# Output projection and second norm with features on partitions, late modulation as columns, residual turned back by VectorE

## The chip, the core and the metric

The kernel runs on one core of one Trainium2 chip. The metric is device time in microseconds (us) of one launch. Engines have their usual names: PE is TensorE, DVE VectorE, ACT ScalarE, POOL GpSimd, SP the engine on whose queue nearly all transfers are issued.

## The reference, cut to what matters

One layer of a residual block for 1024 tokens of 1024 features, float32, with a mixer in front and a SwiGLU behind:

```
mod = silu(c) @ w_ada + b_ada                       # six rows of 1024
shift1, scale1, gate1, shift2, scale2, gate2 = split(mod, 6)
h = rms_norm(x, norm1_w) * (1 + scale1) + shift1
x = x + gate1 * (concat[gated delta rule(h), short conv(h)] @ w_out)    # w_out 1024 x 1024
h = rms_norm(x, norm2_w) * (1 + scale2) + shift2
x = x + gate2 * ((silu(h @ w_gate) * (h @ w_up)) @ w_down)              # 2816 inner features
out = rms_norm(x, norm_f_w)
```

## The kernel before, in words

Every float32 product is made of three passes: each operand is split into a rounded part ("hi", made by ACT) and a rest ("lo", source minus hi, made by DVE), and hi·hi, hi·lo and lo·hi are added in a PSUM bank of 128 x 512. A group of 8 blocks of 128 for the contraction is therefore 24 matmuls.

The program has three stretches.

The **planned stretch** runs from the start to the first half of the output projection. Its steps are tasks in Python threads; `Sim` estimates when each engine could take which step and so writes the order of every queue. Here are the combined projection (`fill`, PE's steady work), the delta rule in two halves of 512 tokens (`gdn`), and the modulation. Of the latter, `ada` and `gate5` make gate1, shift2, scale2 and gate2 as rows: `ada_rows` loads blocks of `w_ada`, adds them up on DVE weighted with `c_act`, and adds over the partitions by two matmuls against `ones`. `w_unit` prepares `w_out`: it multiplies the weight's columns by gate1 and splits. At the end `fill` runs the output projection of the first 512 tokens, with tokens on the partitions of the result: eight groups of 24 matmuls, added to the residual `x2` by `ev_o`. `norm0` saves `x2` to `x2_scr`, takes each token's root mean square by ACT (a sum along the row) and scales.

The **hand-ordered stretch** follows: every engine does its instructions in the order in which the code is written. `w_out_tile(t, ch)` is one group of the projection of the second 512 tokens, `norm_tile` its norm. The SwiGLU wants features on partitions, so the normed rows are turned by PE: `first_half`, `inner_half` and `t_split` write four transposes of 128 x 128 into a bank, ACT takes hi from it, DVE lo.

The SwiGLU's two first products use Strassen-Winograd's seven products in place of eight over halves of tokens, features and columns: the operands of x are B11, B21, B22 and the sums T1 to T4, those of the weights A11, A12, A22 and the sums S1 to S4. `W[p]` holds the weights of pair p of column blocks (11 pairs), `run(p, s)` is step s of a pair: 24 matmuls. Pair 0 (before `for p in range(1, NP)`) also makes the operands from x: `t_split`, `t_high`, `t_low`, `t_sums`, `t_parts`; `part` splits the weights. `block(p, s)` is the other engines' work beside a step. The **third stretch**, the product with w_down, reads `x2` again from `x2_scr`; the change does not touch it.

An instruction that waits holds up all that stands behind it on its engine's queue, transfers on SP's too. Small tiles come from rings: `raw_t` takes one of five tiles of 128 x 512 in turn, so the sixth user waits until the first tile's last reader, which may be a transfer, is through.

Of the kernel before, what the change touches and what calls it, by code (L numbers as in the profile page):

```python
# [51 lines left out]
def kernel(  # L52
# [6 lines left out]
    w_ada: bass.AP,  # L59
    w_mod: bass.AP,  # L60
    b_ada: bass.AP,
# [49 lines left out]
    wada, wout = w_ada[0], w_out[0]  # L111
# [31 lines left out]
    x2_scr = drp.tile([NT, P, D], F32, name="x2_scr", tag="x2_scr")  # L143
    am_scr = drp.tile([NF // 2, 7, P, HT], F32, name="am_scr", tag="am_scr")
# [396 lines left out]
    mod_c = cst.tile([P, 16], F32, name="mod_c", tag="mod_c")  # L541
    s2c = cst.tile([P, KB], F32, name="s2c", tag="s2c")
    b2c = cst.tile([P, KB], F32, name="b2c", tag="b2c")
    db2 = cst.tile([P, 4], F32, name="db2", tag="db2")
    db3 = cst.tile([P, 2], F32, name="db3", tag="db3")
    su = []
# [161 lines left out]
    def setup():  # L708
        sim.wait(lambda: "loads0" in done)
        dma(ct, consts)  # L710
        dma(hv[:, 0:4], A_log[0].partition_broadcast(P))
        dma(hv[:, 4:8], dt_bias[0].partition_broadcast(P))
        wabr = raw((P, KB, 8))
        dma(flat(wabr), w_ab)
        DVE.tensor_copy(row_h, ct[:, 648:652])
# [83 lines left out]
    def h1_load():  # L799
        sim.wait(lambda: "loads0" in done)  # L800
        for j in range(4):
            t = xp.tile([P, 2, HT], F32, name=nm("xt"), tag="x", bufs=8)
            dma(t, x_t[2 * j:2 * j + 2].rearrange("k p c -> p k c"))
            x1t.append(t)
# [130 lines left out]
    def fill():  # L935
# [22 lines left out]
        for ch, us in ((1, us1), (0, us0)):  # L958
            for i in range(4):
                ps = bank(dense, "o")  # L960
                sl = slice(i * P, (i + 1) * P)
                for n, k in enumerate(KORD):
                    sim.wait(lambda: k in us and k in Y[0])
                    for m, (yi, ui) in enumerate(((0, 0), (0, 1), (1, 0))):
                        mm(ps, Y[0][k][yi][:, sl], us[k][ui], n == 0 and m == 0, n == KB - 1 and m == 2)
                sim.spawn(ev_o, PR["evac"], ps, i, ch)

    def ev_o(ps, t, ch):
        cs = slice(ch * HT, (ch + 1) * HT)
        sim.wait(lambda: ("x2", t) in done)  # L970
        DVE.tensor_tensor(x2[t][:, cs], x2[t][:, cs], ps, ALU.add)
        free(ps)
        done.add(("o", t, ch))

    def norm0(t):
        sim.wait(lambda: ("o", t, 0) in done and ("o", t, 1) in done and su and "row" in done and ("g5", 0) in done and ("g5", 1) in done)
        dma(x2_scr[t], x2[t])
        junk = raw((P, D), BF16)
        st = cst.tile([P, 4], F32, name=nm("st"), tag="n2", bufs=4)
        ACT.activation(junk, x2[t], AF.Square, scale=1.0 / 32.0, accum_out=st[:, 0:1])  # L980
        free(junk)
        POOL.tensor_scalar(st[:, 1:2], st[:, 0:1], EPS, None, ALU.add)
        rsqrt_pow(st[:, 2:3], st[:, 1:2], 1)
        DVE.scalar_tensor_tensor(x2[t], x2[t], st[:, 2:3], su[0][:, 0], ALU.mult, ALU.mult)
# [3 lines left out]
    def ada_rows(b, ch, ac=None, get=None):  # L988
        if ac is None:
            ac = wst.tile([P, HT], F32, name=nm("aacc"), tag="aacc", bufs=1)  # L990
        row = get is None
        get = get or raw
        c0 = b * D + ch * HT
        for kk in range(KB):
            r = get()
            dma(r, wada[kk * P:(kk + 1) * P, c0:c0 + HT])
            if kk == 0:
                DVE.tensor_scalar(ac, r, c_act[:, 0:1], None, ALU.mult)
            else:
                DVE.scalar_tensor_tensor(ac, r, c_act[:, kk:kk + 1], ac, ALU.mult, ALU.add)  # L1000
            free(r)
        hl = [raw(dtype=F32R) if row else gt("Tt", (P, HT), F32R) for _ in range(2)]
        esplit(ac, hl[0], hl[1])
        if not row:
            return hl
        ps = bank(chb, "ada")
        mm(ps, ones_r, hl[0], True, False)
        mm(ps, ones_r, hl[1], False, True)
        for t in hl:
            free(t)  # L1010
        return ps

    g5 = {}

    def gate5(ch):
        sim.wait(lambda: len(us0) == KB and len(us1) == KB and "row" in done)
        if 5 not in gates:
            g = gates[5] = wst.tile([P, D], F32, name=nm("gate"), tag="gate", bufs=1)
            dma(g, b_ada[0, 5 * D:6 * D].partition_broadcast(P))
        ac = gt("A", (P, HT)) if ch else None  # L1020
        g5[ch] = ada_rows(5, ch, ac, (lambda: gt("Tt", (P, HT))) if ch else raw)
        done.add(("g5", ch))
        if ch:
            free(ac)

    def ada():
        sim.wait(lambda: 1 in sc_)
        g = wst.tile([P, D], F32, name=nm("gate"), tag="gate", bufs=1)
        dma(g, b_ada[0, 2 * D:3 * D].partition_broadcast(P))
        for ch in range(2):  # L1030
            ps = ada_rows(2, ch)
            DVE.tensor_tensor(g[:, ch * HT:(ch + 1) * HT], g[:, ch * HT:(ch + 1) * HT], ps, ALU.add)
            free(ps)
        gates[2] = g
        for b in (3, 4):
            for ch in range(2):
                ps = ada_rows(b, ch)
                j = (b - 3) * 8 + ch * 4
                diag = wst.tile([P, 4, P], F32, name=nm("diag"), tag="aacc", bufs=1)
                DVE.tensor_tensor(diag, v3(ps, 4), bc1(ident, 4), ALU.mult)  # L1040
                free(ps)
                DVE.tensor_reduce(mod_c[:, j:j + 4], diag, mybir.AxisListType.X, ALU.add)
        DVE.tensor_tensor(mod_c, mod_c, bac[:, 24:40], ALU.add)
        DVE.tensor_copy(b2c, mod_c[:, 0:8])
        DVE.scalar_tensor_tensor(s2c, mod_c[:, 8:16], 1.0, n2c, ALU.add, ALU.mult)
        DVE.tensor_tensor(db2, b2c[:, 4:8], b2c[:, 0:4], ALU.subtract)
        done.add("mods")

    def mod_rows():
        sim.wait(lambda: "mods" in done and ("gdn", 1) in done)  # L1050
        su.append(gt("u", (P, 2, D)))
        for ch in range(2):
            dg = raw((P, 4, P))
            DVE.tensor_tensor(dg, bc1(ident, 4), bc2(s2c[:, 4 * ch:4 * ch + 4], P), ALU.mult)
# [8 lines left out]
            ecopy(su[0][:, 0, ch * HT:(ch + 1) * HT], ps)  # L1063
            free(ps)
        done.add("row")

# [299 lines left out]
    def w_unit(k, ch, take, out_):  # L1366
        r = raw()
        cs = slice(ch * HT, (ch + 1) * HT)
        dma(r, wout[k * P:(k + 1) * P, cs])
        if k < 4:  # L1370
            DVE.scalar_tensor_tensor(r, r, gnc, gates[2][:, cs], ALU.mult, ALU.mult)
        else:
            DVE.tensor_tensor(r, r, gates[2][:, cs], ALU.mult)
        hi, lo = take()
        esplit(r, hi, lo)
# [45 lines left out]
    def w_out_units():  # L1421
        sim.wait(lambda: 2 in gates and "loaded" in done and len(Y[0]) > 5)
# [973 lines left out]
```

## Time and profile before

| | us |
|---|---|
| median of 3 runs | 1159.89 (1158.71 to 1160.67) |
| profiled execution, first to last instruction | 1158.3 |
| PE busy in it | 1148.2 (99%) |
| DVE busy | 961.4 (83%) |
| ACT busy | 565.6 (49%) |
| first matmul of the second half's projection (`w_out_tile(4, 1)`) | 471.55 |
| first matmul of pair 0 / of pair 1 | 520.46 / 564.16 |

The profiled execution's own time isn't given apart; the nearest run lies 0.4 us above its span, the median 1.6 us. Rows of the timeline read: start, duration, engine, line, operation, what it writes<-what it reads, count, and in brackets the idle time before it and what ended that. A row with a count merges instructions that follow each other; they overlap in the pipeline, so the time from one row's start to the next row's start over the count is the cost of one.

### The profile page before, as it was taken

How to read it: one execution, taken by the hardware profiler on the slowest of the kernel's cores; microseconds unless marked ns; L12 is line 12 of the kernel's file. 1: busy time of each engine (PE TensorE's matmuls, PEld its weight loads, DVE VectorE, ACT ScalarE, POOL GpSimd, SP SyncE). 2: the span in 40 equal slices, each digit the busy share in tenths (PEclk: the TensorE clock that was granted, in tenths of full speed). 3: DMA queues.
4: the chain of work that ended last, by engine and by line, in shares of the span. 5: the costliest groups of instructions: out<-in, count | busy, mean ns of one | idle time of the engine just before them, and what ended most of it. 6: DMA issues, size and time to landing. Idle time of an engine off the chain costs nothing.

```text
span 1158.3 us, 16873 instructions
## 1 busy us (share of the span) xinstructions
PE 1148.2 (99%) x5682; PEld 967.1 (83%) x5682; DVE 961.4 (83%) x1820; ACT 565.6 (49%) x1244; POOL 62.3 (5%) x100
## 2 busy tenths in 40 slices
PE   8999999999999999999999999999999999999997
PEld 7888888988888988888888888888888888888886
DVE  7899988999988898669987778877887798688676
ACT  6678732559634543346434443434434455443344
POOL 2110100001101001100000000000000000000002
PEclk9999999999999999999999999999999999999999
DMA  9824456534225546432564457545654599869403
GB/s 363 324 76 143 117 166 174 182 120 138 88 66 164 165 158 210 169 92 72 173 218 163 138 191 231 171 137 175 232 192 143 174 333 394 309 207 337 144 30 146
DMA packets 127544, 209.19 MB, mean 181 GB/s; under 512 B 20577, under 2 KB 45153, under 8 KB 127457
## 3 DMA queue, kind: packets, MB, share of 16 engines
q1 hardware_dynamic: 122080, 204.90, 52.8%
q10 hardware_dynamic: 5376, 3.21, 0.9%
q8 instruction: 45, 0.74, 0.3%
q14 instruction: 43, 0.34, 0.1%
HBM read 153.01 MB, written 55.05 MB: 180 GB/s over the span
## 4 chain that ended last, share of the span: by engine, by line
PE 94%; DVE 3%; ACT 1%; DMA 1%; issue 0%; ACTq 0%; DVEq 0%
PE acc L89 36%; PE acc L448 25%; PE dn L89 17%; PE o L89 4%; PE o L448 3%; PE tr L89 1%; PE K L448 1%; PE A L448 1%; DVE xo L90 1%; PE ab L448 1%; PE w L448 1%; PE u L448 1%; PE kk L448 1%; PE qk L448 1%; DMA raw<-in_w_out_dram 0%; DVE raw L448 0%
## 5 line engine op out<-in xcount | busy, mean ns | idle before, releaser
L448 PE MATMUL acc<-h,u 128*128 128x512 f32 x1200 | 297.9, 397 | 0.0
L448 PEld LDWEIGHTS acc<-h,u 128*128 128x128 f32 x1200 | 220.0, 188 | 42.5 <-issue 0.5
L89 PE MATMUL acc<-h,hl 128*128 128x512 f32 x576 | 135.1, 390 | 0.0
L89 PE MATMUL acc<-T,hl 128*128 128x512 f32 x552 | 130.8, 390 | 0.0
L89 PEld LDWEIGHTS acc<-h,hl 128*128 128x128 f32 x576 | 107.4, 188 | 21.9
L89 PEld LDWEIGHTS acc<-T,hl 128*128 128x128 f32 x552 | 102.4, 188 | 20.4
L90 DVE TENSOR_TENSOR xo<-xo,dn 128x512 f32<-128x512 f32 x84 | 57.0, 684 | 42.3 <-PE dn L89 34.6
L89 PE MATMUL acc<-h,u 128*128 128x512 f32 (+1 forms) x480 | 91.8, 341 | 0.0
L89 PE MATMUL dn<-h,h 128*128 128x512 f32 x396 | 90.7, 389 | 0.0
L89 PEld LDWEIGHTS acc<-h,u 128*128 128x128 f32 x480 | 78.3, 189 | 11.7
L89 PEld LDWEIGHTS dn<-h,h 128*128 128x128 f32 x396 | 74.3, 188 | 15.4
L90 DVE TENSOR_TENSOR cc<-cc,acc 128x512 f32<-128x512 f32 x66 | 41.4, 645 | 32.0 <-PE acc L89 32.0
L448 ACT CAST u<-raw 128x512 fp32r<-128x512 f32 x58 | 35.9, 621 | 56.9 <-PE acc L448 55.1
L448 DVE TENSOR_TENSOR u<-raw,u 128x512 fp32r<-128x512 f32 x82 | 56.1, 685 | 4.0 <-ACT u L448 3.5
L89 PE MATMUL acc<-T,u 128*128 128x512 f32 x240 | 56.0, 389 | 0.0
L448 DVE SCALAR_TENSOR_TENSOR cv<-pr,cols_a,cv 128x512 f32<-128x512 f32 x72 | 53.8, 756 | 0.3
L89 PEld LDWEIGHTS acc<-T,u 128*128 128x128 f32 x240 | 45.1, 188 | 9.3
L90 ACT CAST h<-rw 128x512 fp32r<-128x512 f32 x57 | 32.7, 618 | 41.3 <-PE dn L89 34.6
L90 ACT CAST hl<-S 128x512 fp32r<-128x512 f32 x44 | 25.3, 623 | 56.2 <-DVE S L90 56.2
L90 ACT ACTIVATE cc<-cc 128x512 f32<-128x512 f32 x33 | 20.9, 633 | 64.0 <-DVE cc L90 64.0
L90 ACT CAST u<-R 128x512 fp32r<-128x512 f32 (+1 forms) x60 | 34.2, 585 | 35.3 <-DVE R L90 34.2
L90 DVE TENSOR_TENSOR hl<-S,hl 128x512 fp32r<-128x512 f32 x44 | 28.5, 687 | 26.3 <-ACT hl L90 26.3
(377 smaller groups left out, 2145.1 us busy)
## 6 DMA issues: line engine op xcount, KB each, us to landing
raw<-in_w_in_dram SPq DMA_DIRECT2D x82, 256.0 KB, 3.3
am_scr<-cc SPq DMA_DIRECT2D x77, 256.0 KB, 4.3
raw<-in_w_ada_dram SPq DMA_DIRECT2D x56, 256.0 KB, 3.1
rw<-am_scr SPq DMA_DIRECT2D x55, 256.0 KB, 5.0
rw<-bm_scr SPq DMA_DIRECT2D x53, 256.0 KB, 5.1
bm_scr<-raw SPq DMA_DIRECT2D x51, 256.0 KB, 5.5
R<-in_w_gate_dram SPq DMA_DIRECT2D x22, 512.0 KB, 4.3
R<-in_w_up_dram SPq DMA_DIRECT2D x22, 512.0 KB, 5.5
```

What stands on the lines that cost most here:

```text
L89: return call(*a, **k)
L90: ins = call(*a, **k)
L448: ins = call(*a, **k)
```

## The change

- The output projection is turned: the weight is the stationary operand and y the moving one, so features are on the partitions of the result (`w_out_t(m, b)`; m is a block of 128 features). Still 24 matmuls a group and 8 groups for each 512 tokens.
- gate1, shift2, scale2 and gate2 are made as columns on DVE alone (a product with a running sum, from a transposed `w_mod`), without PE; only gate2 is spread to rows (`row`). gate1 is applied when a group leaves PSUM (`ev_o`, `evict`); `w_unit` only splits.
- The norm now sums over partitions: ACT squares, DVE adds the eight blocks (`sq`), PE adds over partitions by four matmuls with one moving column (`row_sums`), the root is taken on POOL or ACT (`row_root`), a diagonal of it is spread over partitions by a float32 matmul (`row_bc`), and DVE multiplies each block by it (`scale`).
- All of PE's transposes of x are gone (80). Operands are made in the order "scale, hi, lo" block after block (`h_first`, `t_make`).
- The residual is needed with tokens on partitions only at the end. For the first half DVE turns each block in 32 x 32 squares (`turn0`) and four transfers of 32-element runs put the squares in their place in `x2_scr`; for the second half the blocks are saved (`x2t_scr`) and turned one a pair during pairs 2 to 9 (`turn_load`, `turn1`).
- Pair 0 gets an order of its own, with the norm's two short PE steps put between its matmuls (`hooks`).

```diff
-        for ch, us in ((1, us1), (0, us0)):
-            for i in range(4):
...
-                        mm(ps, Y[0][k][yi][:, sl], us[k][ui], n == 0 and m == 0, n == KB - 1 and m == 2)
+        for m in M_ORD:                       # (4, 5, 6, 7, 0, 1, 2, 3)
...
+                    mm(ps, us[k][ui][:, sl], Y[0][k][yi], n == 0 and j == 0, n == KB - 1 and j == 2)
+            sim.spawn(ev_o, PR["evac"], ps, m)
+    def ev_o(ps, m):
+        x_ = x2[m][:, 0:HT]
+        DVE.scalar_tensor_tensor(x_, ps, g1c[:, m:m + 1], x_, ALU.mult, ALU.add)
...
+        ACT.activation(r, x_, AF.Square, scale=1.0 / 32.0)
+        DVE.tensor_tensor(sq_acc[0], sq_acc[0], r, ALU.add)
     def ada():
...
+                    dma(r, w_mod[m, :, b + 2, cs])
+                    DVE.scalar_tensor_tensor(r, r, 1.0, cb[:, cs], ALU.mult, ALU.mult, accum_out=msum[...])
+    def evict(m, ps):
+        add_sq()                              # sq[1] += square of the block before
+        DVE.scalar_tensor_tensor(x2h(m, 1), ps, g1c[:, m:m + 1], x2h(m, 1), ALU.mult, ALU.add)
...
+            ACT.activation(sq_new[0], x2h(m, 1), AF.Square, scale=1.0 / 32.0)
+        dma(x2t_scr[m], x2h(m, 1))
+    def row_sums(hf, b):
+        for t in range(4):
+            pmm(ps[:, t:t + 1], sq[hf][:, t * P:(t + 1) * P], ones[:, 0:1], True, True)
+    def scale(m, hf):
+        DVE.scalar_tensor_tensor(x2h(m, hf), x2h(m, hf), s2c[:, m:m + 1], RSb[hf], ALU.mult, ALU.mult)
+    def halves(src, hi, lo, col=None):
...
+            ACT.activation(hi, src, AF.Identity, bias=col, scale=1.0)
+            DVE.scalar_tensor_tensor(lo, src, col, hi.bitcast(F32), ALU.add, ALU.subtract)
+    def turn0(m):
+        t = raw_t()
+        DVE.transpose(t, x2h(m, 0))
+        for dst, src in rows_of(t, m, 0):     # four
+            dma(dst, src)
+    OB = (4, 5)                               # two banks in turn
+    ps = w_out_t(M_ORD[0], OB[0])
+    row_sums(0, 7)
+    row_root(0)
+    turn0(0)
+    evict(M_ORD[0], ps)
+    ps = w_out_t(M_ORD[1], OB[1])
+    row_bc(0, 6)
+    for m in range(1, 8):
+        turn0(m)
+    evict(M_ORD[1], ps)
+    for i in (2, 3):
+        ps = w_out_t(M_ORD[i], OB[i % 2])
+        for m in range(4 * (3 - i), 4 * (3 - i) + 4):
+            scale(m, 0)
+            h_first(m)
+        evict(M_ORD[i], ps)
+    ps = w_out_t(M_ORD[4], OB[0])
     inner_half(0)
     inner_half(1)
+    for i in range(3):
+        inner_split(i)
+    early_load()
+    evict(M_ORD[4], ps)
+    ps = w_out_t(M_ORD[5], OB[1])
     early_mat(0)
     early_mat(1)
+    evict(M_ORD[5], ps)
...
     for half in (0, 1):
         W[0].load(half)
+    ps = w_out_t(M_ORD[6], OB[0])
+    for n in ("S1", "S2", "S3", "S4"):
+        W[0].sum_n(n)
+    evict(M_ORD[6], ps)
+    ps = w_out_t(M_ORD[7], OB[1])
+    evict(M_ORD[7], ps)
+    add_sq()
+    run0("A11", "B11", b0["X"], True, hooks={12: lambda: row_sums(1, 7), 20: lambda: (row_root(1), row_bc(1, 6))})
+    run0("A12", "B21", b0["Y"], True)
...
+    for k in range(4):
+        scale(k, 1)
+        g0, g1 = x2h(k, 0), x2h(k, 1)
+        DVE.tensor_tensor(g0, g1, g0, ALU.subtract)
+        tm[k] = raw_t()
+        DVE.tensor_tensor(tm[k], x2h(4 + k, 1), g0, ALU.subtract)
+        t_make("T2", k, tm[k], b2c[:, 4 + k:5 + k])
+        if k in (0, 1):
+            part("S2", k)
+    run0("S2", "T2", b0["X"], False, turns=True)
...
     for p in range(1, NP):
...
+                if 2 <= p < 10:
+                    turn_load(p - 2)
+            if s == 1 and 2 <= p < 10:
+                turn1(p - 2)
```

Three places show how the queues change.

DVE's queue of the program before, where the first operands of the SwiGLU are made (`x` is the residual, `o` a group of the projection, `tr` a bank of transposes, `h` the operand, hi and lo):

```order
L90 TENSOR_TENSOR x_4_4595<-x_4_4595,o_5092 128x512
L90 SCALAR_TENSOR_TENSOR x_4_4595<-x_4_4595,st_5119,u_4829 128x1024
L90 SCALAR_TENSOR_TENSOR h_0_945_5130<-tr_5125,b2c,h_0_945_5130 128x512
L90 SCALAR_TENSOR_TENSOR h_0_947_5138<-tr_5133,b2c,h_0_947_5138 128x512
L90 SCALAR_TENSOR_TENSOR h_0_949_5146<-tr_5141,b2c,h_0_949_5146 128x512
L90 SCALAR_TENSOR_TENSOR h_0_951_5154<-tr_5149,b2c,h_0_951_5154 128x512
L90 TENSOR_TENSOR x_5_4596<-x_5_4596,o_5165 128x512
```

The same place on DVE of the changed program, from the last turned block of the first half to the third group's way out of PSUM (`RS` is the spread root, `mod_c` holds the modulation's columns):

```order
L88 STREAM_TRANSPOSE raw_5087<-x_7_4575 128x512
L88 SCALAR_TENSOR_TENSOR x_5_4573<-o_5024,mod_c,x_5_4573 128x512
L88 SCALAR_TENSOR_TENSOR x_4_4572<-x_4_4572,mod_c,RS_5049 128x512
L88 SCALAR_TENSOR_TENSOR h_0_924_5123<-x_4_4572,mod_c,h_0_924_5123 128x512
L88 SCALAR_TENSOR_TENSOR x_5_4573<-x_5_4573,mod_c,RS_5049 128x512
L88 SCALAR_TENSOR_TENSOR h_0_925_5127<-x_5_4573,mod_c,h_0_925_5127 128x512
L88 SCALAR_TENSOR_TENSOR x_6_4574<-x_6_4574,mod_c,RS_5049 128x512
L88 SCALAR_TENSOR_TENSOR h_0_926_5131<-x_6_4574,mod_c,h_0_926_5131 128x512
L88 SCALAR_TENSOR_TENSOR x_7_4575<-x_7_4575,mod_c,RS_5049 128x512
L88 SCALAR_TENSOR_TENSOR h_0_927_5135<-x_7_4575,mod_c,h_0_927_5135 128x512
L88 TENSOR_TENSOR sq_5021<-sq_5021,raw_5094 128x512
L88 SCALAR_TENSOR_TENSOR x_6_4574<-o_5097,mod_c,x_6_4574 128x512
```

Where four "lo" stood behind each other, each lo now stands behind the product that its own hi is made from, with ACT's step between the two; and the group `o_5097` leaves its bank only behind four such turns.

DVE's queue before, at the operands T3 of pair 0:

```order
L90 SCALAR_TENSOR_TENSOR x_4_4595<-raw_5246,db_188,x_4_4595 128x512
L90 SCALAR_TENSOR_TENSOR x_5_4596<-raw_5314,db_188,x_5_4596 128x512
L90 SCALAR_TENSOR_TENSOR x_6_4597<-raw_5395,db_188,x_6_4597 128x512
L90 SCALAR_TENSOR_TENSOR h_1_982_5435<-raw_5437,db_188,h_1_982_5435 128x512
L90 TENSOR_TENSOR R_5445<-R_5445 128x4x128
L90 TENSOR_TENSOR R_5446<-R_5446 128x4x128
L90 TENSOR_TENSOR hl_5632<-R_5445,hl_5632 128x512
L90 TENSOR_TENSOR T_1018_5635<-x_4_4595,T_1018_5635 128x512
L90 TENSOR_TENSOR T_1019_5638<-x_5_4596,T_1019_5638 128x512
```

And in the changed program:

```order
L88 SCALAR_TENSOR_TENSOR x_0_4568<-x_4_4572,db_191,x_0_4568 128x512
L88 TENSOR_TENSOR T_992_5595<-x_0_4568,T_992_5595 128x512
L88 TENSOR_TENSOR hl_5598<-R_5292,hl_5598 128x512
L88 SCALAR_TENSOR_TENSOR x_1_4569<-x_5_4573,db_191,x_1_4569 128x512
L88 TENSOR_TENSOR T_994_5602<-x_1_4569,T_994_5602 128x512
L88 TENSOR_TENSOR hl_5605<-R_5293,hl_5605 128x512
L88 SCALAR_TENSOR_TENSOR x_2_4570<-x_6_4574,db_191,x_2_4570 128x512
L88 TENSOR_TENSOR T_996_5609<-x_2_4570,T_996_5609 128x512
```

The sums of four blocks no longer stand ahead of the four lo; each block's sum and lo follow each other.

SP's queue before, where the hand-ordered stretch begins (`R` are pair 0's weights, `x_scr` the saved residual):

```order
L448 DMA x_scr<-x_1_4592 128x1024
L448 DMA x_scr<-x_2_4593 128x1024
L448 DMA x_scr<-x_3_4594 128x1024
L90 DMA R_5445<-in_w_gate_dram 128x4x256
L90 DMA R_5446<-in_w_up_dram 128x4x256
L90 DMA R_5449<-in_w_gate_dram 128x4x256
L90 DMA R_5450<-in_w_up_dram 128x4x256
```

SP's queue in the changed program, at the same loads (`er` are the early loads of its first columns):

```order
L88 DMA x2t_scr<-x_7_4575 128x512
L88 DMA er_5235<-in_w_gate_dram 128x4x128
L88 DMA raw_5236<-in_w_up_dram 128x4x128
L88 DMA er_5234<-in_w_gate_dram 128x4x128
L88 DMA er_5234<-in_w_up_dram 128x4x128
L88 DMA x2t_scr<-x_0_4568 128x512
L88 DMA x2t_scr<-x_1_4569 128x512
L88 DMA R_5292<-in_w_gate_dram 128x4x256
L88 DMA R_5293<-in_w_up_dram 128x4x256
L88 DMA R_5296<-in_w_gate_dram 128x4x256
L88 DMA R_5297<-in_w_up_dram 128x4x256
```

Before, the four `R` stood right behind the planned stretch's last saved block, and the early loads on ACT's queue; now both stand on SP's, behind saved blocks (`x2t_scr`) of groups that come late in the second half.

More of the change, by code (lines that the diff above doesn't have):

```diff
@@ L986 @@
-    gates = {}
[L988 to L1011, printed above, removed]
@@ L1043, in ada @@
[L1043 to L1051, printed above, removed]
+        cb = wst.tile([P, D], F32, name=nm("cb"), tag="gate", bufs=1)
+        dma(cb, c_scr)
```

510 lines of the change are left out of this document (206 added, 304 removed).

## The prediction, made before the changed kernel ran

> **What bounds the kernel now.** I read the page's busy line and its chain first, then busy time by stretch around the changed part.
>
> ```profile
> PE 1148.2 (99%) x5682; PEld 967.1 (83%) x5682; DVE 961.4 (83%) x1820; ACT 565.6 (49%) x1244; POOL 62.3 (5%) x100
> PE 94%; DVE 3%; ACT 1%; DMA 1%; issue 0%; ACTq 0%; DVEq 0%
> 471.55:520.46 48.91, 48.91 (x230) 40.27 (x228) 31.08 (x50) 20.59 (x39) 4.83 (x10) 1.00 0.28 94
> 520.46:564.16 43.70, 43.70 (x217) 36.60 (x216) 41.00 (x66) 26.52 (x50) 0.76 (x2) 1.00 0.37 117
> 200.00:300.00 100.00, 100.00 (x592) 87.41 (x591) 96.25 (x211) 65.95 (x184) 10.55 (x11) 1.00 0.48 148
> 640.00:1080.00 440.00, 440.00 (x2099) 370.94 (x2098) 353.31 (x567) 190.08 (x357) 0.00 (x0) 1.00 0.65 223
> ```
>
> PE is busy 99% of the time and carries 94% of the chain. So whatever leaves PE shortens the run, as long as nothing else becomes late. The first two windows (length; busy time of PE, its weight loads, DVE, ACT, POOL; clock; DMA) are the hand-ordered projection and pair 0, 92.6 us together. PE never waits in them, but in the second DVE is busy 41.0 of 43.7 us: the queue that the change loads and reorders has 6% to spare there. The others are a part of the planned stretch and the pairs behind, with DVE 96% and 80% busy.
>
> **What leaves PE.** First the transposes.
>
> ```profile
> 528.64 1.91 PE L89 MATMUL tr<-ident,raw 128*128 128x128 f32 x16
> 530.30 2.98 PE L89 MATMUL acc<-h,hl 128*128 128x512 f32 x12
> 533.12 2.17 PE L89 MATMUL tr<-ident,x 128*128 128x128 f32 x16
> 535.05 5.72 PE L89 MATMUL acc<-T,hl 128*128 128x512 f32 x24
> 540.60 2.89 PE L89 MATMUL acc<-h,hl 128*128 128x512 f32 x12
> 477.15 1.10 PE L89 MATMUL row<-Tt,ones 128*128 128x512 f32 x4
> 478.08 2.96 PE L89 MATMUL o<-h,WQ 128*128 128x512 f32 x12
> L448 PE MATMUL ada<-raw,ones x12: 392/395/478, 141.1 to 292.3; 128*128 128x512 f32 x12
> L448 PE MATMUL RS<-raw,ones x2: 592/592/592, 62.6 to 63.0; 128*128 128x512 f32 x2
> L448 PE MATMUL G<-g,ct x8: 177/262/263, 84.9 to 99.2; 128*128 128x16 f32 x8
> ```
>
> Sixteen transposes take 528.64 to 530.30 = 1.66 us, in one case 1.93. The 80 are five such lots: 4 x 1.66 + 1.93 = 8.6 us. The four `row` matmuls of gate2 take 0.93, or 0.23 each; they stay under another form (the diagonal of gate2), four for four, and the four early `row` matmuls for scale2 go. The 12 `ada` matmuls go: 12 x 0.23 = 2.8. Off PE: 8.6 + 2.8 + 0.9 = 12.3 us.
>
> Added are two spreads of the root in float32, each two records like RS, 0.43 between their starts: 2 x 0.9 = 1.8; and eight row sums, 16 records of one column, nearest in shape to G, whose records hold at least a weight load of about 0.19 (none shows the time for this width): 16 x 0.19 = 3.0 at most, 16 x 0.09 = 1.4 at least, 2.2 taken. Net off PE: 12.3 - 4.0 = 8.3 us. The projection keeps its 16 x 24 matmuls; exchanging stationary and moving operand costs nothing that a row shows. Were PE still the bound, that would be the answer. It is not the one I give, since its operands now come through a chain.
>
> **The chain DVE, ACT, DVE.** These three forms, a product with RS, hi with a bias, and lo, are already in the kernel for the first norm, so they have rows.
>
> ```profile
> L448 DVE SCALAR_TENSOR_TENSOR hf<-xt,s1c,RS x8: 743/746/752, 64.3 to 76.9; 128x512 f32<-128x512 f32 x8
> L448 ACT ACTIVATE h<-hf,b1c x8: 709/720/727, 65.0 to 78.3; 128x512 fp32r<-128x512 f32 x8
> L448 DVE SCALAR_TENSOR_TENSOR h<-hf,b1c,h x8: 745/748/752, 66.8 to 79.0; 128x512 fp32r<-128x512 f32 x8
> 72.78 0.74 DVE L448 SCALAR_TENSOR_TENSOR hf<-xt,s1c,RS 128x512 f32<-128x512 f32 x1
> 73.57 0.72 ACT L448 ACTIVATE h<-hf,b1c 128x512 fp32r<-128x512 f32 x1
> 78.27 0.72 ACT L448 ACTIVATE h<-hf,b1c 128x512 fp32r<-128x512 f32 x1
> 79.02 0.75 DVE L448 SCALAR_TENSOR_TENSOR h<-hf,b1c,h 128x512 fp32r<-128x512 f32 x1
> 529.99 2.73 DVE L90 SCALAR_TENSOR_TENSOR T<-tr,b2c,T 128x512 fp32r<-128x512 f32 x4
> 552.67 2.43 ACT L90 CAST T<-raw 128x512 fp32r<-128x512 f32 x4 [1.28 <-DVE raw L90]
> 551.96 2.49 DVE L90 TENSOR_TENSOR raw<-x,raw 128x512 f32<-128x512 f32 x4
> L448 DVE STREAM_TRANSPOSE Tt<-xbd x8: 669/669/705, 202.8 to 374.3; 128x512 f32<-128x512 f32 x8
> L448 POOL TENSOR_TENSOR rk<-nk,nhalf x8: 1007/1216/1445, 114.7 to 318.4; 128x4 f32<-128x4 f32 x8
> ```
>
> Independent DVE instructions follow each other at (2.73 - 0.74) / 3 = 0.66 us for a two-scalar product (called STT here) and (2.49 - 0.69) / 3 = 0.60 for a plain one; ACT ends 0.03 before its DVE reader starts, DVE 0.05 before its ACT reader. In `h_first` a block is therefore 0.74 + 0.05 + 0.72 + 0.03 + 0.66 = 2.2 us, of which 0.8 is DVE waiting for ACT. Four blocks and the group's way out of PSUM (0.60 + 0.66) are 10.1 us; a group of 24 matmuls is 540.60 - 535.05 = 5.55, elsewhere a little less; 5.5 taken. The projection has two banks, so PE must wait for DVE.
>
> I now follow DVE from the first matmul of the second half's projection, time 0 here (471.55 before), to pair 1's (92.6 before).
>
> *To the end of `evict` 1.* Group 0 ends at 5.5, the row sums at 6.6 to 8.5; then DVE 0.2, POOL's power 1.2, DVE's diagonal, with gaps: 9. Eight turns at 0.60 follow, but `raw_t` has five tiles, one held by the diagonal. The sixth turn waits for the first's transfers, the eighth for the third's.
>
> ```profile
> 120.33 1.76 SPq L448 DMA_DIRECT2D dl<-L  x4
> 121.50:122.50 1.00, 1.00 (x6) 0.83 (x5) 1.00 (x7) 1.00 (x4) 0.18 (x1) 1.00 0.23 33
> DMA to landing us min/median/max: 2.2/3.2/4.4
> ```
>
> Four transfers of 128-byte runs take SP 1.76 us to issue; 33 GB/s at 0.23 of the engines would be 143 at all of them, 1.8 us for a block's 256 KB. The last row is that of `xbd`, 64 KB in the same runs. So: first turn done at 9.8, issues to 11.6 and the saved block to 12.0, third block's issues to 15.5, landed at 18, `evict` 1 done at 19.3. With transfers that cost nothing it would be 15.
>
> *`h_first`.* 8 x 2.2 + 2 x 1.26 = 20.2: 39.5. PE ends group 3 at 24.8 and waits for its bank till 29.4, again some 4.6 us for the next.
>
> *Inner operands and early weights.* Six plain half-width steps, six lo behind ACT, two ways out: 5.0 + 1.3. The early loads reuse the inner operands' tile, so they start at 45 and land at 49; two hi and lo and `evict` 5: 51.3. With the loads hidden 48.5.
>
> *The weights of pair 0.* They stand on SP behind the saved block of `evict` 5.
>
> ```profile
> R<-in_w_gate_dram SPq DMA_DIRECT2D x2, 512.0 KB, 4.5
> R<-in_w_up_dram SPq DMA_DIRECT2D x2, 512.0 KB, 5.0
> 520.71 0.50 SPq L90 DMA_DIRECT2D R<-in_w_up_dram  x1
> 526.59 0.68 DVE L90 TENSOR_TENSOR S<-R,R 128x512 f32<-128x512 f32 x1
> ```
>
> Issued at 51.6 to 53.1, the third (which S1 needs) lands at about 57.8 and the fourth at 59; before, the last was issued at 520.71 and S1 ran by 526.59. Eight sums end at 64. Only behind them stand `evict` 6 and 7, with a square on ACT (0.63, the hi's length less bias) and an addition between: 5 us, 69. PE has ended group 7 at 57 and twelve matmuls of pair 0 at 59.7 and waits for that sum of squares: 9 us. If the loads hid, 62.
>
> *Pair 0.* Row sums, eight matmuls, the spread: 73. B22's scales, lo and S4's parts: 6.3. T2: two dependent sums per block, so 0.77 + 2 x 0.71 + 0.05 + 0.72 + 0.03 + 0.66 = 3.65, and 0.6 more for two weight parts: 15.8. T1 and S1: 3.6. T3: 2.1 a block and two parts, 9.6. T4 9.4. End on DVE 117.7; PE's last 15 matmuls 3.4: **pair 1 starts at 121, not 92.6: +28.4**.
>
> Ahead of time 0 only `ada` counts: -2.8 (its four `row` for scale2, -0.9, also ran before 471.55, where the four for gate2 now stand; the four at 477.15 lie inside the 92.6). DVE there does 64 products with sums where it did 64 without, loses the 16 products of gate1 into `w_out` and the four diagonals, gains eight additions; PE is busy throughout, so I cost this at nothing; cover gone, it is at most 14 x 0.6 = 8 us on either side.
>
> *Pair 1.* DVE enters it late: 18 steps (10.9 us) still stand ahead of its S1 and S2.
>
> ```profile
> 564.16 5.60 PE L89 MATMUL acc<-h,hl 128*128 128x512 f32 x24
> 567.21 1.21 DVE L90 TENSOR_TENSOR S<-R,R 128x1024 f32<-128x1024 f32 x1
> 570.42 1.29 DVE L90 TENSOR_TENSOR hl<-S,hl 128x512 fp32r<-128x512 f32 x2 [0.74 <-ACT hl L90]
> ```
>
> Before, S1 began 3.0 us after the pair and its lo 6.3. Now S1 begins 9.5 after and the lo 12.8, while PE wants it two groups in, at 11; with the later steps' margins +3 (0 to 6). From pair 2 on each pair adds one turn of 0.60 and four transfers to 38 us in which DVE is 80% busy: nothing, and with the cover gone 8 x 0.6 = 4.8.
>
> The clock: PE now idles.
>
> ```profile
> 1154.00:1158.00 4.00, 0.00 (x0) 0.00 (x0) 0.39 (x1) 0.36 (x1) 0.00 (x0) 0.55 0.52 194
> L89 PE MATMUL ps<-raw,ones x4: 1057/1057/1219, 3.8 to 6.5; 128*128 128x512 f32 x4
> ```
>
> Behind 4 us without matmuls the granted clock reads 0.55, and RS's form took 1057 ns early in the run against 592 warm. A slow PE behind the first two waits is absorbed by the next wait; behind the third it delays the spread by one or two us: +1 (0 to 4).
>
> The Trainium skill ("TensorE: Matmul & The Clock Gate", Part 1) says that an idle window of about 3.4 us halves the clock until as long a busy one. By it each wait over 3.4 us would lose 1.7 us of PE work; only the third is on the path, so the sum would be 1 us higher. The 0.55 agrees; no wait of this length in mid-run is in this trace.
>
> **The sum.** 28.4 - 2.8 + 3 + 1 = +29.6. The span 1158.3 becomes 1187.9; the median lies 1.6 above the span: 1189.5, **1189**.
>
> Bounds. With the three DMA waits gone (19.3 to 15, 51.3 to 48.5, 69 to 64 counted from there: -4, -3, -5), no debt in pair 1 and no clock loss: -16, 1173. With transfers at half rate (+5), R later by 3, clock +4, pair 1 +6: 1203.
>
> **The rivals.**
>
> *DVE's loops alone, DMA hidden.* For it: every wait of DMA in the windows above is off PE's path now. Against: the ring of five and SP's order are in the code. 1173, and less where ACT runs ahead more than I see: 1166.
>
> *PE stays the bound (the other side).* The place is the two banks: if four blocks of hi and lo took no longer than the 5.5 us of a group, everything behind would fit: between the row sums and T4's last lo DVE has 55 plain steps, 44 STT, 8 turns and 12 half-width ones (0.37), 33 + 29 + 5 + 4 = 71 us, against PE's 15 groups and 4 us, 86. Price: 8.3 us off, 1151.5. It decides at 1.4 us a block; the forms' rows say 2.2. It would need lo not to wait for its own hi.
>
> *Transfers and clock cost more.* 2048 short writes a block were never queued so densely here; if they run at half rate and pair 1 passes its debt on, 1198 to 1206.
>
> *The change doesn't do what it says* where the planned stretch, reordered, lets PE wait: DVE's 96% from 200 to 300 would be the place; the gain of 2.8 then becomes a loss of up to 8, inside the upper range.
>
> **How the numbers follow.** The forecast's case, 1180 to 1197, gets 0.58; the hidden DMA 1166 to 1180, 0.19; dearer transfers and clock 0.13 (up to 1206); PE the bound, about 1151, 0.06; something between it and 1166, 0.04. Within 0.2% (2.3 us, about what a measurement can tell from no change) lies next to none of these: 0.02; slower 0.92, faster 0.06. The range 1167 to 1203 leaves out the last two cases and the ends of the next, 0.15.
>
> **What would show it.** In the profile after: PE idle of 4 to 5 us twice in the projection's fourth to sixth group, ended by DVE's way out of the bank; one of about 9 us at the second `ss`, ended by DVE's `sq`; waits of one to two us inside T2, T3 and T4, ended by DVE; idle DVE before each `h` lo ended by ACT, about 0.8 us; the eighth STREAM_TRANSPOSE waiting for a DMA; no `tr` in the second half's projection or pair 0; pair 2 and later as before. I am wrong if PE stays busy through the projection, if R lands before DVE asks for it, or if the time goes elsewhere.

## The result, and the profile after

The changed kernel takes 1195.49 us (median; 1194.61 to 1195.92) against 1160.13 for the kernel before, a ratio of 1.0305 with a 95% interval of 1.0291 to 1.0320. The forecast was 1189, range 1167 to 1203. The profiled execution spans 1193.8 us, 35.5 more than before.

The busy line and the chain of the page after:

```profile
PE 1154.7 (97%) x5606; PEld 964.9 (81%) x5606; DVE 956.2 (80%) x1882; ACT 565.3 (47%) x1238; POOL 55.7 (5%) x85
PE 85%; DVE 7%; ACT 3%; DMA 2%; issue 1%; POOL 1%; SPq 0%; ACTq 0%; DVEq 0%
```

PE has 76 instructions fewer and is busy 6.5 us longer. That isn't more work: part of it ran at a lower clock, as the next view shows (clock 0.91 and 0.86). The chain now takes 7% from DVE, 3% from ACT and 2% from transfers.

Busy time by stretch: the second half's projection, pair 0, and a stretch of 440 us in the pairs behind (length; PE, its weight loads, DVE, ACT, POOL; clock; DMA):

```profile
470.64:528.96 58.32, 50.49 (x203) 39.59 (x202) 32.19 (x55) 14.45 (x25) 1.01 (x1) 0.91 0.48 115
528.96:599.66 70.70, 51.17 (x179) 37.29 (x178) 50.87 (x80) 28.56 (x49) 0.00 (x0) 0.86 0.12 40
674.50:1114.50 440.00, 440.00 (x2099) 370.94 (x2099) 357.71 (x574) 189.77 (x357) 0.00 (x0) 1.00 0.69 231
```

The first two were 48.91 and 43.70 us and are 58.32 and 70.70, 36.4 more together; in both PE waits and its clock is below 1. The first matmul of the first comes 0.9 us earlier (470.64 for 471.55): 36.4 - 0.9 = 35.5, the whole difference. From pair 1 to the end the time is as before.

Who waited for whom from 470 to 600, PE first, then DVE (total, times, longest):

```profile
PE ss L87 <- DVE sq L88: 8.0, 1, 8.0
PE o L87 <- DVE x L88: 7.8, 3, 5.0
PE acc L87 <- ACT cc L88: 4.1, 1, 4.1
PE acc L87 <- ACT T L88: 3.2, 3, 1.5
PE acc L87 <- ACT hl L88: 2.9, 1, 2.9
DVE h L88 <- ACT h L88: 9.3, 9, 2.3
DVE T L88 <- ACT T L88: 8.7, 12, 0.8
DVE S L88 <- DMA R<-in_w_gate_dram: 7.4, 1, 7.4
DVE raw L88 <- DMA x_scr<-raw: 2.5, 2, 1.4
```

PE's waits are those forecast, for its bank (`o`, 7.8), for the sum of squares (`ss`, 8.0) and inside T2 to T4, and one that was not: 4.1 us for ACT's copy of a bank (`cc`). DVE, for which PE waits, waits itself: 18 us for its own hi by ACT, 7.4 for R, 2.5 for the ring of raw tiles.

The rows of the timeline at which the steps of the forecast can be read:

```profile
488.30 0.71 DVE L88 STREAM_TRANSPOSE raw<-x 128x512 f32<-128x512 f32 x1 [1.38 <-DMA x_scr<-raw]
488.94 0.71 DVE L88 SCALAR_TENSOR_TENSOR x<-o,mod_c,x 128x512 f32<-128x512 f32 x1
494.04 0.75 DVE L88 SCALAR_TENSOR_TENSOR h<-x,mod_c,h 128x512 fp32r<-128x512 f32 x1 [0.79 <-ACT h L88]
500.51 4.85 PE L87 MATMUL o<-WQ,h 128*128 128x512 f32 x12 [4.98 <-DVE x L88]
510.57 4.60 PE L87 MATMUL o<-WQ,h 128*128 128x512 f32 x12 [2.42 <-DVE x L88]
528.76 0.69 DVE L88 TENSOR_TENSOR S<-R,R 128x512 f32<-128x512 f32 x1 [7.45 <-DMA R<-in_w_gate_dram]
538.99 0.69 DVE L88 TENSOR_TENSOR sq<-sq,raw 128x512 f32<-128x512 f32 x1 [0.76 <-ACT raw L88]
539.83 1.84 PE L87 MATMUL ss<-ones,sq 128*128 128x1 f32 x8 [7.96 <-DVE sq L88]
541.53 3.76 PE L87 MATMUL acc<-h,hl 128*128 128x512 f32 x8
547.85 1.28 ACT L88 ACT_TABLE_LOAD   x1
550.00 0.75 DVE L88 SCALAR_TENSOR_TENSOR h<-x,mod_c,h 128x512 fp32r<-128x512 f32 x1 [2.27 <-ACT h L88]
592.45 7.37 PE L87 MATMUL acc<-T,hl 128*128 128x512 f32 x24 [4.13 <-ACT cc L88]
599.66 5.60 PE L87 MATMUL acc<-h,hl 128*128 128x512 f32 x24
```

The last row is pair 1. Four windows of the clock, around the first of PE's waits and around the sum of squares:

```profile
496.00:500.50 4.50, 0.00 (x0) 0.00 (x0) 3.47 (x6) 0.93 (x2) 0.00 (x0) 0.68 0.63 131
500.50:503.00 2.50, 2.49 (x6) 2.01 (x7) 1.71 (x3) 1.33 (x2) 0.00 (x0) 0.50 0.28 105
540.00:542.00 2.00, 2.00 (x9) 2.00 (x10) 0.00 (x1) 0.30 (x2) 0.00 (x0) 0.50 0.00 0
542.00:545.00 3.00, 3.00 (x8) 2.32 (x8) 1.47 (x3) 0.96 (x2) 0.00 (x0) 0.50 0.00 0
```

Behind both waits PE runs at half its clock for some microseconds: eight matmuls take 3.6 us (541.53 to 545.09).

### The profile page after: what moved, and what is told of

It reads as the page before. It is cut to its first block, busy times and chain, and to the rows that moved or that the text cites. A ratio compares the mean times of both kernels' runs of the same rounds, so it can differ in the third digit from the quotient of the medians.

```text
span 1193.8 us, 16835 instructions
## 1 busy us (share of the span) xinstructions
PE 1154.7 (97%) x5606; PEld 964.9 (81%) x5606; DVE 956.2 (80%) x1882; ACT 565.3 (47%) x1238; POOL 55.7 (5%) x85
## 4 chain that ended last, share of the span: by engine, by line
PE 85%; DVE 7%; ACT 3%; DMA 2%; issue 1%; POOL 1%; SPq 0%; ACTq 0%; DVEq 0%
PE acc L87 33%; PE acc L448 24%; PE dn L87 17%; PE o L448 4%; DVE x L88 1%; PE A L448 1%; PE K L448 1%; DVE h L88 1%; DVE raw L88 1%; ACT T L88 1%; DVE hl L88 1%; DVE xo L88 1%; PE w L448 1%; PE u L448 1%; PE qk L448 1%
## 5 line engine op out<-in xcount | busy, mean ns | idle before, releaser
L87 PE MATMUL acc<-T,hl 128*128 128x512 f32 x552 | 138.5, 403 | 11.3 <-ACT cc L88 4.1
L87 PEld LDWEIGHTS acc<-T,hl 128*128 128x128 f32 x552 | 105.0, 194 | 37.1 <-ACT T L88 5.1
L448 ACT CAST u<-raw 128x512 fp32r<-128x512 f32 x69 | 42.8, 620 | 63.4 <-PE acc L448 58.0
L448 DVE SCALAR_TENSOR_TENSOR raw<-raw,cb 128x512 f32<-128x512 f32 x64 | 43.6, 682 | 3.9 <-DMA raw<-in_w_mod_dram 3.8
```

The source lines that it names most:

```text
L87: return call(*a, **k)
L448: ins = call(*a, **k)
```

## The experiments

Theory: DVE's queue in the hand-ordered stretch sets when pair 1 starts, through the order in which its steps stand and not through their amount; PE only waits. Rivals: the two PSUM banks, the transfers, the longer DVE work as such, the late turns. Times are medians; differences are against the 1195.5 of the changed kernel unless another is named.

One thing limits what a difference of an us or two says. In the profiled executions of the changed kernel and its twelve variants the projection's first matmul came at 468.0 to 471.0 us, although none of the edits touches the code of the planned stretch. Where it matters, the way from that matmul to pair 1's first is therefore given too: 129.0 us in the changed kernel, 92.6 in the kernel before.

**Six banks** (`e1_banks`).

```diff
-    OB = (4, 5)
+    OB = (4, 5, 2, 3, 0, 1, 4, 5)
```

> The changed kernel with six PSUM banks in turn for the second half's projection in place of two; nothing else differs. My theory (DVE's queue sets the end of pair 0, PE only waits for it): PE no longer waits in the projection (5.0 + 2.4 us gone there) but waits that much longer at the second sum over partitions; the time stays at 1195.5, within 1.5 us, pair 1 starts within 1.5 us of 599.7. Rival (the two banks themselves cost the time): 6 to 7 us faster, about 1189.

1195.48: no difference. PE's wait at the sum of squares:

```profile
PE ss L87 <- DVE sq L88: 19.2, 1, 19.2
```

PE runs ahead through the projection and waits 19.2 us in one place. The banks were where PE waited, not why.

**lo one block behind hi** (`e2_pipe`, then `e5_casts`).

```diff
-            scale(m, 0)
-            h_first(m)                        # hi on ACT, lo on DVE
+        for k in range(5):                    # T2, T3 and T4 likewise
+            if k < 4:
+                scale(m0 + k, 0)
+                h_high(m0 + k)
+            if k:
+                h_low(m0 + k - 1)
```

> The changed kernel with each lo put one block behind its hi (the first operands, T2, T3 and T4), so that DVE makes the next block's product while ACT makes this block's hi. Theory: about 0.8 us of DVE waiting per block goes, less a remainder where the next product is shorter than ACT's step: 6 us in the first operands, 2.9, 2.7 and 2.7 in T2, T3 and T4, 14 us in all, time 1180 to 1183. Rival (the transfers set the end, R above all): the time before T2 does not move, 8 us in all or less, 1187 or more.

1184.85: 10.6 us faster, more than the rival allows and less than 14 (the way to pair 1 is 118.6 us, 10.4 shorter). DVE's waits for ACT in this run:

```profile
DVE hl L88 <- ACT hl L88: 6.2, 9, 1.3
DVE h L88 <- ACT h L88: 3.2, 2, 2.3
```

Those for `h` fell from 9.3 to 3.2 and those for `T` from 8.7 to nothing. But waits for the weights' parts (`hl`) rose from 2.1 to 6.2: each part's hi now stood on ACT behind the next operand's. So the next kernel issues it ahead:

```diff
     def t2_sum(k):
+        if k in (0, 1):
+            W[0].cast("S2", k)                # S3, A22 likewise; only the lo stays behind
```

> The kernel with lo one block behind hi (run before at 1184.9), and now also the hi of the weights' parts S2, S3 and A22 issued on ACT ahead of the operand's hi of the same block, not behind the next one. In that run DVE still waited about 0.6 us for ACT's hi at each of these six parts. Theory: the six waits go, 3.0 to 3.6 us, time 1181 to 1182. Rival (PE, not DVE, is now last in T2 to T4): no gain, 1184 or more.

1179.38, another 5.5 us; the waits for `hl` fell by 3.4 to 2.8. PE's wait for ACT's copies (`cc`) is 1.2 shorter as well (2.7 for 3.9). The way to pair 1 is 114.6 us, 4.0 shorter than in the run before; the rest of the 5.5 is in neither trace. By the medians 16.1 us came from nothing but the order of hi and lo, by the way to pair 1 14.4.

**The turns directly ahead of each block's scaling** (`e3_ring`).

```diff
-    for m in range(1, 8):
-        turn0(m)
...
+            turn0(m)
             scale(m, 0)
             h_first(m)
```

> The changed kernel with each of the first half's turned blocks (a DVE turn and its four transfers of 128-byte runs) put directly ahead of the scaling of the same block, in place of eight turns in a row; the DVE work is the same. Theory (the eight turns wait 4 us for their ring of five tiles): 4 us less on DVE's queue, 1191 to 1192. Rival (the short transfers themselves are the limit, wherever they stand): no gain, since the same 32 transfers must land before the early weights behind them on SP; 1195 or more.

1194.68 (1193.4 to 1196.8): less than 1 us, a miss. Two of its four executions took 1193.4 and 1193.5 at a mean granted clock of 0.987 and 0.986, two 1195.9 and 1196.8 at 0.984; the rows are of the one of 1195.9. The theory was right on the ring (no transfer holds up a turn any more) and overlooked what the turns had covered:

```profile
482.30 0.75 DVE L88 SCALAR_TENSOR_TENSOR x<-o,mod_c,x 128x512 f32<-128x512 f32 x1 [3.04 <-PE o L87]
485.98 0.70 DVE L88 STREAM_TRANSPOSE raw<-x 128x512 f32<-128x512 f32 x1
486.72 0.75 DVE L88 SCALAR_TENSOR_TENSOR x<-x,mod_c,RS 128x512 f32<-128x512 f32 x1
488.26 0.75 DVE L88 SCALAR_TENSOR_TENSOR h<-x,mod_c,h 128x512 fp32r<-128x512 f32 x1 [0.79 <-ACT h L88]
```

Without them DVE idles 3.0 us until the second group is out, and each later turn adds 0.74 to a block without covering ACT's 0.8, since it stands ahead of the product and not between it and lo. Gone are 4.0 us of waiting (2.5 for transfers, 1.5 for the tile that the root's diagonal holds), new are 3.0. The net of 1.0 is about what was measured.

**Pair 0's weights ahead of two saved blocks on SP** (`e4_rload`).

```diff
-        dma(x2t_scr[m], x2h(m, 1))            # evict 4 and 5
+        held.append(m)
...
     for half in (0, 1):
         W[0].load(half)
+    for m in held:
+        dma(x2t_scr[m], x2h(m, 1))
```

> The changed kernel with the two saved blocks of the fifth and sixth group moved on SP's queue from ahead of pair 0's first weights to behind them; DVE's order is the same. Theory (the weights wait on the queue behind a block that DVE finishes late): R is issued at about 516 in place of 521.8, S1 starts at about 523 in place of 528.8, the wait at the second sum over partitions shrinks from 8.0 to about 3 us, time 5 us lower, 1190 to 1191. Rival (the weights' memory comes free no earlier, or DVE has no time for the sums there): no change.

1192.07 (1190.9 to 1195.2), 3.4 us by the median, less than the 5 expected. The profiled execution is the slowest of the four, 1195.2. SP's queue and DVE's first sum in it:

```profile
515.75 0.45 SPq L88 DMA_DIRECT2D R<-in_w_gate_dram  x1
526.38 0.69 DVE L88 TENSOR_TENSOR S<-R,R 128x512 f32<-128x512 f32 x1 [4.73 <-DMA R<-in_w_gate_dram]
R<-in_w_gate_dram SPq DMA_DIRECT2D x2, 512.0 KB, 8.6
```

R was issued 6.0 us earlier (515.75 for 521.77), yet the sum began only 2.4 earlier: the loads from `w_gate` took 8.6 us to land in place of 4.9, now right behind the early weights' loads. So the theory had half of it: the queue's order delayed R, but it took the landing to be as long as before, and there most of what was gained at the issue was lost again. The rival's causes are out: R's memory was free, and DVE idled 4.7 us ahead of the sums. PE's wait for the sum of squares fell from 8.0 to 5.2, not to 3. In this execution even the 2.4 us were mostly lost behind it: pair 1 starts at 599.12 (599.66 in the changed kernel), since PE's last 24 matmuls took 8.05 us for 7.21. The three shorter executions have no trace.

**The end of pair 0** (`e6_tail`).

```diff
+    ACT.activation(warm, ones[:, 0:1], AF.Silu)   # right behind the root
     part("S4", 0)
...
     for k in range(4):
         DVE.tensor_tensor(tm[k], x2h(4 + k, 0), tm[k], ALU.subtract)
-        t_make("T4", k, tm[k])
+        t_high("T4", k, tm[k])
+    for k in range(4):
+        t_low("T4", k, tm[k])
```

> The changed kernel with three edits of the end alone: ACT loads its table for silu right behind the root (it did so behind a copy, ahead of the B22 operands' hi, where DVE waited 2.3 us); the hi of T4 and A22 are made ahead of all their lo, so that ACT reaches its copy of X earlier; S3 times T3 goes block by block. Theory: 1.4 to 2 us from the table, 3 from the last 24 matmuls, which stood behind that copy and ended 7.2 us after it; T4's waits (2.7) go too: 6.5 to 7.5 us in all, 1188 to 1189. Rival (pair 1's start is bound by its own weights or by DVE's work behind the pair): 2 us or less, 1193 or more.

1188.85, 6.6 us by the median, as expected. But its trace, 7.8 us shorter than the changed kernel's, has only 5.2 of that where the edits are (the way to pair 1 is 123.8 us); the other 2.6 lie ahead of the projection (468.00 for 470.64), and the edits don't explain them. So the theory's 6.5 to 7.5 was somewhat too much. The wait of 2.27 at the first B22 operand fell to 0.75: 1.5 of it was ACT's table load with the small instruction that calls for it, for which the forecast had no term.

**Without the late turns** (`e7_noturn`).

```diff
-        dma(x2t_scr[m], x2h(m, 1))
+        dma(x2_scr[4 + m // 2][:, m % 2 * HT:(m % 2 + 1) * HT], x2h(m, 1))
...
-                if 2 <= p < 10:
-                    turn_load(p - 2)
-            if s == 1 and 2 <= p < 10:
-                turn1(p - 2)
```

> The changed kernel without the late turns of the second half's residual in pairs 2 to 9: left out are eight loads, eight turns by DVE and 32 transfers of 128-byte runs; the eight blocks are stored unturned, so that the output's second half is not the reference's. Theory (hidden beside PE): no change, 1195.5 within 1 us. Rival (each pair pays its turn): 4.8 us faster, 1190.7.

1195.59 (1194.1 to 1198.1): no difference. Eight turns and 32 transfers of short runs beside a busy PE cost nothing that shows.

**All remedies** (`e8_all`).

The edits above but the plain `e3_ring`, and two that were not tried alone:

```diff
-                scale(m0 + k, 0)
+                turn0(m0 + k)
+                scale(m0 + k, 0)              # and then, one block late, h_low
...
-    for n in ("S1", "S2", "S3", "S4"):
-        W[0].sum_n(n)
     evict(M_ORD[6], ps)
...
     add_sq()
+    W[0].sum_n("S1")
+    W[0].sum_n("S2")                          # S3 and S4 behind the root's diagonal
```

> All at once: lo one block behind hi with the parts' hi ahead; the first half's turns inside that alternation, where they fill DVE's wait; pair 0's weights ahead of the saved blocks on SP; six PSUM banks for the projection; the weights' sums behind the last groups' way out of PSUM; the early silu table; T4's hi ahead of its lo and S3 times T3 block by block. Theory (DVE's queue set the end, and its waits were 30 us of it): first operands end some 8 us earlier, no wait of PE at the second sum over partitions (8 us) except what R's landing leaves, T2 to T4 8 us shorter, 7 at the end: 1159 to 1166. Rival (the change's cost is in the longer DVE work itself or the transfers): 1172 or more.

1160.24, a ratio to the kernel before of 1.0004 (0.9994 to 1.0013): all of the 35 us is gone, with the same products, sums, turns and transfers. PE's waits in the stretch:

```profile
PE acc L87 <- DVE hl L88: 2.4, 1, 2.4
PE acc L87 <- DVE T L88: 0.7, 1, 0.7
PE acc L87 <- ACT cc L88: 0.5, 1, 0.5
```

So the price was the order. (The six banks, which alone brought nothing, belong to this version too; it was not run without them.) The edits are not additive one by one (0 + 16.1 + 0.8 + 3.4 + 6.6 = 26.9): in the combination the turns stand among other blocks' products, where they cover ACT, and the weights' sums no longer stand ahead of the sum of squares. How much each of these two brings was not measured apart.

**PE kept busy through its longest wait** (`e10_heat`).

```diff
-hooks={12: lambda: row_sums(1, 7),
+hooks={12: lambda: (heat(34), row_sums(1, 7)),
```

> The changed kernel with 34 matmuls more, into a free bank, in the place where PE waits 8.0 us for the second sum over partitions; their result isn't used. They add 7.8 us of PE work and nothing else. If the wait's only price is the wait, the time stays at 1195.5 within 1 us. If PE's clock after the wait costs time on the path (behind it 8 row sums took 1.7 us against 0.8 in the first half, and 8 matmuls 3.6 against 1.9), the spread comes 2 to 3 us earlier and the time is 1192.5 to 1194.

Unclear: 1194.15, but its four times are 1191.9, 1192.2, 1196.1 and 1196.2. The mean granted clock goes with them: 0.990 and 0.992 in the two shorter executions, 0.987 in the two longer ones. Only a longer one has a trace (1196.2). In it the sum of squares came 1.9 us behind the last added matmul, and the clock fell all the same:

```profile
537.00:539.00 2.00, 0.22 (x1) 0.00 (x0) 1.24 (x2) 1.25 (x3) 0.00 (x0) 1.00 0.30 112
539.00:541.00 2.00, 1.86 (x9) 1.89 (x10) 0.00 (x0) 0.28 (x2) 0.00 (x0) 0.61 0.06 22
541.00:543.00 2.00, 2.00 (x6) 1.52 (x6) 1.47 (x3) 0.97 (x2) 0.00 (x0) 0.50 0.00 0
```

So some 4 us go with the clock in this kernel, but that the shorter executions were spared the fall at this place is likely and not shown. The clock's cost on the path is read from the rows of the changed kernel (below).

**Beyond the kernel before** (`e9_late`, `e12_dve`, `e11_pool`).

```diff
+    for m in (4, 5, 6, 7, 0, 1, 2, 3):
+        dma(x2t_scr[m], x2h(m, 0))            # first half too, in place of turn0
...
+            if s == 3 and 2 <= p < 10:
+                turn1(p - 2)                  # a second turn a pair
```

> The version with all remedies (1160.2, equal to the kernel before) with three more: the first half's residual is saved unturned at once and turned in pairs 2 to 9 as well (a second turn a pair), so that its eight turns leave DVE's queue ahead of pair 0; the weights' sums stand between the last groups' ways out of PSUM; both parts S2 are made ahead of the first T2 operand, for which PE waited 2.4 us. Theory (DVE is still last there, PE waits 3.6 us in pair 0, and DVE has room in the pairs): pair 1 starts 2 to 4 us earlier, 1156 to 1158, faster than the kernel before. Rival (two turns a pair are too many, or R's landing is last): 1160 or more.

1159.18, ratio 0.9998 (0.9989 to 1.0007): not faster than before, a miss by 1 us. PE's rows at pair 0's third product show what is left of its waits, and a fall of the clock:

```profile
536.67 0.49 PE L87 MATMUL acc<-T,hl 128*128 128x512 f32 x1 [0.56 <-ACT T L88]
538.69 1.87 PE L87 MATMUL acc<-T,hl 128*128 128x512 f32 x6 [1.53 <-DVE T L88]
541.46 5.06 PE L87 MATMUL acc<-T,hl 128*128 128x512 f32 x11 [0.90 <-DVE T L88]
538.00:541.00 3.00, 1.87 (x6) 1.05 (x6) 2.93 (x5) 0.95 (x2) 0.00 (x0) 0.83 0.00 0
541.00:544.00 3.00, 2.54 (x6) 2.08 (x7) 2.87 (x5) 3.00 (x7) 0.00 (x0) 0.50 0.00 0
```

Three waits of 3.0 us together, and at a clock of 0.50 the last 11 matmuls took 5.06 us. The fall of the clock is not why the version missed, though: this execution took 1160.0 at a mean clock of 0.995, but four of the eleven have 0.998 or 0.999, as the kernel before, and took 1158.5 to 1159.7. That leaves the waits, and the next version is made to shorten them.

```diff
-            W[0].cast("S2", k)                # next tile of the ring
+        own("S2", q, f"T4_{q}")               # a tile of its own, made ahead of the spread
```

> The last version (1159.2, equal to the kernel before) with the weights' parts S2 and S1 in tiles of their own (those of T4, still unused), so that both S2 are made while DVE waits for the second root's spread, and ACT's copy of X behind the second of T3's sums. Theory (PE waits 3.0 us in pair 0's third product for DVE, and its clock falls to 0.66 there): 1.2 us less on DVE between the spread and T1, 1 us less at T3, and less time at the lower clock: 2 to 4 us, 1155 to 1157. Rival (PE's order and not DVE is last by now): 1158.5 or more.

1157.17, ratio 0.9979 (0.9970 to 0.9988): faster than the kernel before, by 0.2%. Its rows at the same place:

```profile
536.64 1.65 PE L87 MATMUL acc<-T,u 128*128 128x512 f32 x6 [1.13 <-DVE T L88]
539.41 2.79 PE L87 MATMUL acc<-T,u 128*128 128x512 f32 x11 [1.12 <-DVE T L88]
538.00:541.00 3.00, 1.88 (x9) 1.33 (x8) 2.87 (x5) 2.27 (x5) 0.00 (x0) 1.00 0.00 0
```

Waits of 2.25 us are left, the clock stays at 1.00, and the last 11 matmuls take 2.79 us, 2.3 less. All eleven executions have a mean clock of 0.998 or 0.999; the last version's four at that clock took 2 us more, so the gain is the order's and not the clock's. The tiles of their own and the later copy of X were not tried apart.

The next version makes these lo on POOL, each on POOL's own queue right behind its hi:

```diff
-        own_low("S2", q, DVE)                 # S1 likewise
+        own_low("S2", q, POOL)
```

> The same with the four lo of S2 and S1 on POOL, which is idle there, in place of DVE. Theory: 1.2 us less on DVE again in T1; 0 to 2 us below the version with DVE, 1153 to 1157. Rival (POOL is so slow at 128 x 512, no row shows it, or holds up DVE, that its lo come late): slower than the version with DVE by more than 1 us.

1159.27, ratio 0.9997 (0.9988 to 1.0006): the rival was right. POOL's two lo and DVE's two sums beside them:

```profile
518.46 3.31 POOL L88 TENSOR_TENSOR u<-S,u 128x512 fp32r<-128x512 f32 x2 [40.83 <-ACT u L88]
518.87 3.46 DVE L88 TENSOR_TENSOR R<-R,S 128x512 f32<-128x512 f32 x2
```

POOL takes 1.65 us for a lo that DVE makes in 0.60 (no row shows POOL with DVE idle), and DVE's two sums took 3.46 us beside it; the same two took 1.29 in the version with DVE. They stand ahead of the root: counted from the projection's first matmul, DVE took up the spread 1.3 us later than there, and pair 1 began 1.4 later (92.9 us for 91.4). The rest of the 2.1 us between the medians is not in that stretch.

## Why the prediction was right, point by point

All times count from the projection's first matmul (470.64 after).

- *The two DMA waits and `h_first`.* `evict` 1 ended at 19.0 (19.3 said), `h_first` with its ways out at 39.9 (39.5), `evict` 5 at 50.7 (51.3). PE's wait for its bank was 5.0 and 2.4, where 4.6 twice was said: behind the first wait 12 matmuls took 4.7 us at the lower clock, which absorbed part of the second. Of DVE's 4.0 us of waiting among the turns 2.5 was for transfers, which the forecast charged with all of it; 1.5 was for the root's spread, which had still to read the diagonal's tile.
- *R behind a saved block.* S1 could begin at 58.1 (57.8), the sum of squares ended at 69.0 (69). PE came at 61.2, not 59.7, so its wait was 8.0 for 9.
- *T2, T1, T3, T4.* 15.8, 3.6, 9.4 and 9.3 us, against 15.8, 3.6, 9.6 and 9.4.
- *The clock term was too small.* Said was +1. Row sums took 1.7 us for 0.8, and eight matmuls 3.6 for 1.9: 2.6, and DVE could read the spread at 75.7 in place of 73. The 1.7 us worked out beside the term would have been too small as well.
- *A term was missing.* From the spread to T2 it took 8.3 us for 6.3: ACT's table load of 1.28 us stood ahead of the first hi, behind a copy that waits for PE, and DVE waited 2.27 us for that hi.
- *Another was too small.* Behind DVE's last lo stood 24 matmuls, not 15, since they begin with a copy of the bank that stands on ACT's queue behind T4's hi; and they ran partly at the lower clock: 7.0 us for 3.4.
- *One term pulled the other way.* Pair 1 was to pay +3 for DVE's late start and paid nothing: the kernel is 35.5 us late at pair 1's first matmul and 35.5 at the end.
- *A gain was too large.* Ahead of time 0 it was 0.9, not 2.8: the reordered planned stretch makes PE wait 1.8 us anew, in the stretch that the fourth rival named though not between 200 and 300, as the waits before 470 show. These waits differ from trace to trace; in the variants' traces time 0 lies at 468.0 to 471.0, so the gain there is 0.6 to 3.6.

```profile
PE P L448 <- DVE qs L448: 0.9, 1, 0.9
PE tr L448 <- ACT x L88: 0.6, 1, 0.6
PE acc L448 <- ACT pr L448: 0.3, 1, 0.3
```

Sum: from time 0 to pair 1 +28.4 became +36.4 (2.7 at the spread, 2.0 at the table, 3.6 at the end, -0.3 in the stages between); with -0.9 that is 35.5 for the 29.6 said. So DVE's path was read rightly, in its order and in nearly every step, and PE's end of it was not. The 3 us charged to pair 1 hid part of that: without them the forecast would have missed by 9 us in place of 6, which is luck.

The rival "DVE's loops alone" fell, since R's landing and the ring showed as waits on DVE's path. "Transfers and clock cost more" was right on the clock alone, and the time stayed below its 1198. "PE stays the bound" named the right point: hi and lo of a block would have to take no longer than PE's share. With lo taken off its own hi's heels that is nearly reached, and the gain is 2.5 us rather than 8.3: in the best version PE still waits 3.8 us between 469 and 605. In its trace 2.6 us are gained ahead of the projection, 1.2 from there to pair 1, and 0.6 lost behind.

## What to carry to other kernels

Where two engines hand a block back and forth in order (product on DVE, hi on ACT, lo on DVE), put another block's work between the hand-over and the return: here that order alone, of the same instructions, was worth 14 to 16 us. Work that is moved off the bottleneck engine is worth its time only if what it leaves there still arrives in time, so read the queue of the engine that must now deliver, and ask what each moved step had covered. A small step that changes engines at a junction (a table load, a bank's copy, a weights' load behind a store) can cost its full length there, whatever its share of the whole.

## What the runs showed of the hardware that had not been expected

- PE's clock falls without one long wait, and not in every execution. In the trace of `e9_late` waits of 0.56 and 1.53 us, with matmuls between and behind, came ahead of the fall (0.98 from 539 to 540, 0.50 from 540 to 541), and the one of 0.90 only behind it; in four of that kernel's eleven executions the mean clock shows no fall. Two waits of 1.13 and 1.12 in `e12_dve` brought none in any of eleven. In the trace of `e10_heat` a wait of 1.91 us with eight one-column row sums behind it did. The Trainium skill ("TensorE: Matmul & The Clock Gate", Part 1) names one idle window of about 3.4 us; these runs show that a stretch of that length need not be wholly idle.
- DVE is held up beside POOL: its two sums of two operands took 2.2 us longer beside POOL's lo (3.46 for 1.29). The Trainium skill ("SBUF — State Buffer", Who interferes with whom) says that a DVE instruction with two inputs in SBUF and a GpSimd instruction that reads SBUF exclude each other, and that the later one blocks; the two rows agree for DVE, and whether POOL was blocked too no row shows.
- Loads of 512 KB that were issued 6.0 us earlier let DVE start only 2.4 us earlier: those from `w_gate` took 8.6 us to land right behind the early weights' loads, and 4.9 where these had landed. Which of the transfers beside them held them up was not tested.
